# Turning the attention's q and k by VectorE blocks and DMA in place of TensorE transposes

## The chip, the core and the metric

The kernel runs on one core of one Trainium2 chip. The metric is the time of one launch on the device, in microseconds (us). The kernel before took 700.55 us (median of three runs, 700.42 to 700.56).

## What is computed

One layer over 512 tokens and 1024 channels in float32. The input is normalised and multiplied by one wide weight matrix; its columns are split among an mLSTM branch, a stick-breaking attention branch and the merge gates. Both branches are projected back, merged by the gates, and put through an output product.

```python
h = rmsnorm(x, norm_w)
proj = jnp.einsum('bsd,de->bse', h, w_in) + b_in
(mq, mk, mv, mi, mf, mo, mz, sq, sk, sv, sz, gates) = jnp.split(proj, split_at, axis=-1)
...
qs = rmsnorm(to_heads(sq, SB_HEADS), sb_q_norm_w)
ks_ = rmsnorm(to_heads(sk, SB_HEADS), sb_k_norm_w)
os_ = stick_breaking_attention(qs, ks_, to_heads(sv, SB_HEADS))
y_s = os_.transpose(0, 2, 1, 3).reshape(b_, s_, SB_WIDTH) * jax.nn.silu(sz)
...
merged = (g_m * jnp.einsum('bse,ed->bsd', y_m, w_proj_m)
          + g_s * jnp.einsum('bse,ed->bsd', y_s, w_proj_s))
x = x + jnp.einsum('bsd,de->bse', merged, w_out)
```

The attention has 8 heads of 128 channels. Its scores need q and k with the channel on the partitions (the contraction runs over partitions), while the input product leaves the tokens of q and k on the partitions. The turn from one to the other is what the change is about.

## The kernel before

**Units.** The dense work is a list of 118 units; the loop at L1199 runs them in order. A unit is one 512 KB piece of weights and its 24 matmuls: every product is made of three (`mm3`, L84), since both factors are split in a high and a low part. Two units ahead, `ahead` splits the weights: ACT copies the high part `wh` (L90), DVE subtracts to get the low part `wl` (L91). SP issues the loads of `stg`, four units ahead (L110), into three buffers. Around the two halves of a unit's matmuls the loop puts the evacuation of the unit before, functions put off with `defer(n, fn)` (they come up n units later), and one step of each active head. In the units listed in `REST` (11, 16, 20, 23, 24, ...) no head takes a step.

**Order of the groups.** The attention comes in two sets of four heads. Set 0: q in units 0 to 3, k 4 to 7, v 8 to 11, z 12 to 15. Set 1: q 16 to 19, k 20 to 23, z 24 to 27, v 28 to 31. Then two mLSTM pairs, pair 0 in units 32 to 51 (o, z, v, q, k) and pair 1 in 52 to 71, then gates, the two projections and the last product. A q or k group fills four PSUM banks (`dps`, one for each block of 128 tokens, of which there are four); after its fourth unit DVE moves the banks to `qraw` or `kraw` (L335, 128 tokens x 512 channels each), ACT squares them for the norm (`sqj`, L344), POOL makes the reciprocal root `rk` or `rq` (L267, L268), and DVE scales `kraw` by it (L355). There are four `dps` banks in all, so the next group's first matmul into a bank waits for that move.

**A head** (`head`, L383) is a generator: each `yield` ends a step. Step one turns q and k of the head with 8 TensorE transposes into PSUM (`aps`, L389) and splits them in high and low parts (L393, L394, L90, L91). The later steps make scores, weigh them (ACT sigmoids, POOL masks, DVE scans at L422 and products at L423 into `a_all`), transpose the weights in square blocks of 32 on DVE (`ay`, L440), move the blocks to their places with 16 DMAs issued by SP (`az<-ay`, L458), split them (`ath`, `atl`) and multiply them with v. A head begins when its unit in `SB_START` is reached and its set's k is marked done.

**Buffers.** `a_all` and `ay` share the tag "A", which has four buffers used in turn: a head's two tiles stand at two places, and the next but one head gets them again. Whoever fills a buffer waits for all who still read what was in it before; for `ay` these are its 16 `az` DMAs.

Of the kernel before, what the change touches and what calls it, by code (L numbers as in the profile page):

```python
# [34 lines left out]
def tile_hybrid_layer(  # L35
# [20 lines left out]
    def pool(name, bufs=1, **k):  # L56
# [11 lines left out]
    BUFS = {"stg": 3, "wh": 3, "wl": 3, "tmp": 2, "acc": 1, "om": 3, "P5": 2, "A": 4,  # L68
            "qk": 18, "vh": 5, "vl": 5, "y": 16, "brow": 1}

    MISC = {"om", "tmp", "acc", "brow", "stg"}

    def blk(tag, dt=F32, shape=(512,), name=None, p=128):

        where = mp if tag in MISC else sp
        return where.tile([p] + list(shape), dt, name=name or tag, tag=tag, bufs=BUFS[tag])

    def dense_ps():
# [233 lines left out]
    class SbSet:  # L312
        def __init__(self, s):
            self.s = s
            self.raw = {"q": [], "k": []}
            self.r = []
            self.v = []

        def z_group(self):
# [10 lines left out]
        def qk_group(self, name, c0):  # L330
            row = []

            def evac(tb, ps):
                t = blk("qk", name=name + "raw")
                nc.vector.tensor_tensor(t, ps, row[0], op=OP.add)  # L335
                self.raw[name].append(t)

                def norm():
                    ssq = tiny.tile([128, 4], F32, name="ssq", bufs=2)
                    rr = tiny.tile([128, 8], F32, name="r" + name, bufs=8 if name == "q" else 4)  # L340
                    r = rr[:, 0:4]
                    junk = blk("acc", BF, (128,), name="sqj")
                    for h in range(4):
                        nc.scalar.activation(junk, t[:, h * 128:(h + 1) * 128], AF.Square,  # L344
                                             accum_out=ssq[:, h:h + 1])
                    rstd(r, ssq, 128, EPS)
                    if name == "q":
                        rn = rr[:, 4:8]
                        nc.gpsimd.tensor_scalar(rn, r, -1.0, None, op0=OP.mult)
                        self.r.append((r, rn))  # L350
                    else:
                        def scale():
                            for h in range(4):
                                hs = slice(h * 128, (h + 1) * 128)
                                nc.vector.tensor_scalar(t[:, hs], t[:, hs], r[:, h:h + 1], None, op0=OP.mult)  # L355
# [27 lines left out]
        def head(self, h):  # L383
            hs = slice(h * 128, (h + 1) * 128)
            tr = []
            for name in ("q", "k"):
                tp = att_ps()
                for tb in range(TB):
                    nc.tensor.transpose(tp[:, tb * 128:(tb + 1) * 128], self.raw[name][tb][:, hs], ident)  # L389
                th = blk("qk", FR, name=name + "th")  # L390
                tl = blk("qk", FR, name=name + "tl")
                if name == "q":
# [4 lines left out]
                tr.append((th, tl))  # L397
            yield
# [217 lines left out]
    class MPair:  # L616
# [25 lines left out]
        def qk_group(self, name, c0, o):  # L642
            def evac(ct, ps):
# [12 lines left out]
                def mult():  # L656
# [3 lines left out]
                    def high():  # L660
                        th = blk("qk", FR, name="m%sh" % name)
                        tl = blk("qk", FR, name="m%sl" % name)
                        nc.scalar.activation(th, t, AF.Copy)
# [157 lines left out]
    for p in pairs:  # L821
        p.o_group()
        p.z_group()
        p.v_group()
        p.qk_group("q", C_MQ, 0)
        p.qk_group("k", C_MK, 8)

    gs_t, gm_t = [], []

    def gs_tile(ct):  # L830
        tag = ("brow", "om", "om", "acc", "qk")[min(ct, 4)]
        gs_t.append(blk(tag, shape=(516 if tag == "om" else 512,), name="gs")[:, 0:512])
        return gs_t[ct]

    def gm_tile(ct):
        gm_t.append(blk("qk", name="gm"))
        return gm_t[ct]
# [47 lines left out]

    merged = []

    def pm_evac(ct, ps):
# [3 lines left out]
        th = blk("y", FR, name="mgh")  # L892
        tl = blk("qk", FR, name="mgl")
        nc.scalar.activation(th, t, AF.Copy)
# [196 lines left out]
    def first_split(i, low=None):  # L1091
        u = units[i]
        for j in range(2):
            hi, lo = blk("qk", FR, name="fh"), blk("y", FR, name="fl")
            nc.scalar.activation(hi, u.st[:, j, :], AF.Copy)
# [12 lines left out]

    idle = blk("qk", FR, name="idle")
    nc.vector.memset(idle.bitcast(F32), 0.0)  # L1110
# [139 lines left out]
```

## Time and profile before

| | before |
|---|---|
| runs, median of 3 | 700.55 us (700.42 to 700.56) |
| the profiled execution's own time | 700.42 us |
| span of its profile | 698.7 us |
| POOL busy, instructions | 109.2 us, 249 |
| DMA moved | 80.94 MB in 104759 packets |
| `az<-ay` DMAs | 128 of 40 KB, 2.0 us to landing |

The profile is of one execution. A row of its timeline has the start in us from the span's beginning, the time taken, the engine, the line, the operation, what it writes and reads, and how many neighbours were merged; in brackets stands the idle time of the engine before it and who ended that. PE is TensorE, DVE is VectorE, ACT is ScalarE, POOL is GpSimd, SP is the engine that issues most DMAs. The chain of work that ended last is followed back from the last instruction: what stands on it sets the end. The 1.7 us between span and the execution's own time lie outside the profile.

### The profile page before, as it was taken

Reading aid. Unit: us, or ns where it says so; the run is one execution under the profiler, and the core shown is the slowest. Engines: PE = TensorE matmul, PEld = TensorE weight load, DVE = VectorE, ACT = ScalarE, POOL = GpSimd, SP = SyncE. Lnnn points to the kernel's source line nnn. Section 1 sums busy time; section 2 is a strip of 40 time slices with the busy share of each in tenths; the row PEclk is TensorE's granted clock in tenths of the full one; section 3 lists DMA queues with packets and bytes.
Section 4 is the critical chain, followed back from the end, with each engine's and each line's share of the span. In section 5 each row is a group of like instructions: output and inputs, shape, how many; then the busy total and the mean of one; then the engine's idle time right before and its main releaser. Section 6 shows DMA issues by size and latency. Waiting matters only on the chain.

```text
span 698.7 us, 9267 instructions
## 1 busy us (share of the span) xinstructions
PE 690.4 (99%) x3220; PEld 575.2 (82%) x3220; DVE 463.5 (66%) x807; ACT 335.6 (48%) x629; POOL 109.2 (16%) x249
## 2 busy tenths in 40 slices
PE   7999999999999999999999999999999999999997
PEld 5888888888888888888888888888888888888876
DVE  6837887856787775389944738995343364445996
ACT  6245354475554543244475534446563353344451
POOL 5422122252130220000011120001111000111021
PEclk9999999999999999999999999999999999999999
DMA  7432424525433444333332244433323456589434
GB/s 247 136 106 71 126 63 123 148 59 145 112 107 84 130 109 137 90 95 94 97 98 67 61 108 120 120 90 91 91 61 86 112 157 219 144 184 208 126 81 130
DMA packets 104759, 80.94 MB, mean 116 GB/s; under 512 B 6766, under 2 KB 89096, under 8 KB 104712
## 3 DMA queue, kind: packets, MB, share of 16 engines
q1 hardware_dynamic: 102552, 74.45, 37.2%
q0 software_dynamic: 2016, 5.77, 4.5%
q8 instruction: 25, 0.41, 0.2%
q14 instruction: 22, 0.18, 0.1%
q10 hardware_dynamic: 144, 0.13, 0.1%
HBM read 65.12 MB, written 2.10 MB: 96 GB/s over the span
## 4 chain that ended last, share of the span: by engine, by line
PE 97%; DMA 1%; DVE 1%; POOL 0%; SPq 0%; issue 0%; ACT 0%; DVEq 0%
PE dps L85 27%; PE dps L86 27%; PE dps L87 27%; PE aps L86 3%; PE aps L87 3%; PE aps L85 3%; PE aps L389 1%; PE dps L1139 1%; PE dps L1137 1%; PE dps L1138 1%; DMA stg<-in_w_in_dram 1%; PE aps L760 1%; PE aps L762 1%; PE aps L761 1%; DVE fl L1096 0%; POOL fl L1096 0%
## 5 line engine op out<-in xcount | busy, mean ns | idle before, releaser
L91 DVE TENSOR_TENSOR wl<-stg,wh 128x1024 fp32r<-128x1024 f32 x92 | 112.6, 1223 | 112.9 <-ACT wh L90 111.3
L85 PE MATMUL dps<-hh,wh 128*128 128x512 f32 x448 | 175.2, 391 | 0.0
L87 PE MATMUL dps<-hh,wl 128*128 128x512 f32 x448 | 174.5, 389 | 0.0
L86 PE MATMUL dps<-hl,wh 128*128 128x512 f32 x448 | 174.5, 389 | 0.0
L90 ACT ACTIVATE wh<-stg 128x1024 fp32r<-128x1024 f32 x92 | 96.8, 1052 | 58.4 <-PE dps L87 38.2
L87 PEld LDWEIGHTS dps<-hh,wl 128*128 128x128 f32 x448 | 84.1, 188 | 17.8
L85 PEld LDWEIGHTS dps<-hh,wh 128*128 128x128 f32 x448 | 84.1, 188 | 17.1 <-DVE tmp L372 0.4
L86 PEld LDWEIGHTS dps<-hl,wh 128*128 128x128 f32 x448 | 84.2, 188 | 16.9
L85 PE MATMUL dps<-wh,hh 128*128 128x512 f32 x224 | 88.2, 394 | 0.1
L87 PE MATMUL dps<-wh,hl 128*128 128x512 f32 x224 | 87.3, 390 | 0.0
L86 PE MATMUL dps<-wl,hh 128*128 128x512 f32 x224 | 87.3, 390 | 0.0
L87 PEld LDWEIGHTS dps<-wh,hl 128*128 128x128 f32 x224 | 42.0, 188 | 9.0
L85 PEld LDWEIGHTS dps<-wh,hh 128*128 128x128 f32 x224 | 42.1, 188 | 8.6 <-issue 0.5
L86 PEld LDWEIGHTS dps<-wl,hh 128*128 128x128 f32 x224 | 42.1, 188 | 8.1
L651 DVE SCALAR_TENSOR_TENSOR acc<-tmp,vec,acc 128x511 f32<-128x511 f32 (+2 forms) x48 | 36.0, 750 | 1.7
L654 ACT ACTIVATE tmp<-acc 128x512 f32<-128x512 f32 x16 | 10.1, 633 | 50.8 <-DVE acc L651 50.8
L422 DVE TENSOR_TENSOR_SCAN om<-om 128x512 f32<-128x512 f32 (+3 forms) x32 | 26.7, 835 | 8.8 <-POOL om L416 8.8
L416 POOL TENSOR_SCALAR_AFFINE_SELECT om<-om 128x128 f32<-128x128 f32 x32 | 14.1, 441 | 109.0 <-ACT om L414 109.0
L713 POOL TENSOR_SCALAR_AFFINE_SELECT w_all<-om 128x128 f32<-128x128 f32 x16 | 6.0, 412 | 153.9 <-DVE om L708 136.8
L414 ACT ACTIVATE om<-aps,rq 128x512 f32<-128x512 f32 (+3 forms) x32 | 16.8, 525 | 22.8 <-PE aps L87 22.8
L85 PE MATMUL dps<-yh,wh 128*128 128x512 f32 x64 | 24.9, 389 | 0.0
L86 PE MATMUL dps<-yl,wh 128*128 128x512 f32 x64 | 24.9, 389 | 0.0
(271 smaller groups left out, 1225.3 us busy)
## 6 DMA issues: line engine op xcount, KB each, us to landing
stg<-in_w_in_dram SPq DMA_DIRECT2D x87, 512.0 KB, 3.8
az<-ay SPq DMA_DIRECT2D x128, 40.0 KB, 2.0
stg<-in_w_proj_s_dram SPq DMA_DIRECT2D x8, 512.0 KB, 3.7
B<-in_w_out_dram SPq DMA_DIRECT2D x8, 512.0 KB, 4.8
stg<-in_w_proj_m_dram SPq DMA_DIRECT2D x8, 512.0 KB, 3.6
wl<-stg POOLq DMA_DIRECT2D x8, 512.0 KB, 5.5
brow<-in_b_in_dram SPq DMA_DIRECT2D x8, 256.0 KB, 4.0
hz<-ht SPq DMA_DIRECT2D x64, 32.0 KB, 1.9
```

The costliest lines, as they stand in the source:

```text
L85: nc.tensor.matmul(ps, ah, bh, start=first, stop=False)
L86: nc.tensor.matmul(ps, ah, bl, start=False, stop=False)
L87: nc.tensor.matmul(ps, al, bh, start=False, stop=last)
L90: nc.scalar.activation(hi, src, AF.Copy)
L91: nc.vector.tensor_tensor(lo, src, hi.bitcast(F32), op=OP.subtract)
L389: nc.tensor.transpose(tp[:, tb * 128:(tb + 1) * 128], self.raw[name][tb][:, hs], ident)
L414: nc.scalar.activation(om[:, 0:n], zp, AF.Sigmoid, scale=rn[:, h:h + 1])
L416: nc.gpsimd.affine_select(out=om[:, ts], in_=om[:, ts], compare_op=OP.is_gt, fill=1.0, base=0, channel_multiplier=1, pattern=[[-1, 128]])
L422: nc.vector.tensor_tensor_scan(back, back, back, 1.0, op0=OP.mult, op1=OP.bypass)
L651: nc.vector.scalar_tensor_tensor(acc[:, j:], t[:, 0:T - j], cw(3 - j, ch), acc[:, j:], op0=OP.mult, op1=OP.add)
L654: nc.scalar.activation(t, acc, AF.Sigmoid)
L760: nc.tensor.matmul(nm[:, 0:258], ph, vh, start=j == 0, stop=False)
```

## The change

For q of both sets and k of set 1 (`TURNED`) the TensorE transposes go. In their place a new function `turn` runs for each of the four token blocks: two DVE transposes in square blocks of 32 write into two tiles `ty` of the tag "A"; after the fourth block, 32 DMAs of 32 KB carry the blocks to their places in `tz`, eight in each of four units that follow. In set 0 SP issues them all, in set 1 SP and POOL issue half each. The head then reads `tz` where it read PSUM; q is multiplied by the norm weight in place, once for two heads. k of set 0 keeps its TensorE transposes. The heads of set 1 begin in units 31, 33, 36, 39 in place of 26, 28, 31, 34 (the first one waits for k to be marked done, in unit 32), and pair 0's v group comes behind its q and k. The tag "qk" now has buffers of twice the size, half as many.

```diff
-SB_START = [10, 13, 16, 19, 26, 28, 31, 34]
+SB_START = [10, 13, 16, 19, 31, 33, 36, 39]
+TURNED = {("q", 0), ("q", 1), ("k", 1)}
...
-            "qk": 18, "vh": 5, "vl": 5, "y": 16, "brow": 1}
+            "qk": 9, "vh": 5, "vl": 5, "y": 16, "brow": 1}
...
+                        if tb % 2:
+                            defer(1, lambda: self.turn(name, tb - 1))
+                            defer(1, lambda: self.turn(name, tb))
...
-                            if tb == TB - 1:
+                            if (name, self.s) in TURNED:
+                                self.turn(name, tb)
+                            elif tb == TB - 1:
                                 done.add(("k", self.s))
...
+        def turn(self, name, tb):
+            if tb == 0:
+                self.ty[name] = [sp.tile([128, 8, TB, 32], F32, name="ty", tag="A", bufs=4) for _ in range(2)]
+            ty = self.ty[name]
+            for g in range(2):
+                nc.vector.transpose(ty[g][:, :, tb, :],
+                                    self.raw[name][tb][:, 256 * g:256 * g + 256].rearrange("p (x j) -> p x j", j=32))
+            if tb < TB - 1:
+                return
+            tz = self.tz[name] = [None, None]
+            def move(g, bs):
+                if tz[g] is None:
+                    tz[g] = blk("qk", F32, (2, 4, 128), name="tz")
+                src = ty[g].rearrange("p (h b) i j -> p b h (i j)", h=2)
+                for b in bs:
+                    for a in range(4):
+                        q = nc.gpsimd if self.s and a % 2 else nc.sync
+                        q.dma_start(tz[g][32 * b:32 * b + 32, :, a, :], src[32 * a:32 * a + 32, b])
+                if name == "k" and g == 1 and bs[-1] == 3:
+                    defer(2, lambda: done.add(("k", self.s)))
+            for n, (g, bs) in enumerate([(0, (0, 1)), (0, (2, 3)), (1, (0, 1)), (1, (2, 3))]):
+                defer(1 + n, lambda g=g, bs=bs: move(g, bs))
...
+                if (name, self.s) in TURNED:
+                    tp = self.tz[name][h // 2][:, h % 2].rearrange("p a (i j) -> p i a j", j=32)
+                    th, tl = [x.rearrange("p (i a j) -> p i a j", a=4, j=32) for x in own]
+                    if name == "q" and h % 2 == 0:
+                        z = self.tz[name][h // 2]
+                        nc.vector.tensor_scalar(z, z, qkw, None, op0=OP.mult)
+                else:
+                    tp = att_ps()
+                    for tb in range(TB):
+                        nc.tensor.transpose(tp[:, tb * 128:(tb + 1) * 128], self.raw[name][tb][:, hs], ident)
...
-        p.v_group()
+        if p.p:
+            p.v_group()
         p.qk_group("q", C_MQ, 0)
         p.qk_group("k", C_MK, 8)
+        if not p.p:
+            p.v_group()
```

Below, rows are in each engine's program order; a number behind a name tells tiles apart, and what an instruction waits for stands in brackets (DMAHW: a lane of DMAs issued by SP, DMASW: one of those issued by POOL).

The first place is DVE's queue in units 22 and 23. In it are the first block transposes of head 3's weights (`ay`), the scans and products behind them, the low part of unit 25's weights, and the first move of set 1's k out of PSUM. Before:

```order
L91 TENSOR_TENSOR atl_1688<-az_1372,ath_1687 128x384 [waits Activation_49]
L440 STREAM_TRANSPOSE ay_1699<-a_all_1612 128x4x32 x4
L440 STREAM_TRANSPOSE ay_1699<-a_all_1612 128x4x32 [waits DVE_49]
L422 SCALAR_TENSOR_TENSOR om_1709<-om_1709 128x256 [waits Pool_49]
L423 TENSOR_TENSOR a_all_1612<-a_all_1612,om_1709 128x256 [waits DVE_49,Pool_49]
L422 SCALAR_TENSOR_TENSOR om_1719<-om_1719 128x384 [waits Pool_49]
L423 TENSOR_TENSOR a_all_1612<-a_all_1612,om_1719 128x384 [waits DVE_49,Pool_49]
L91 TENSOR_TENSOR wl_1742<-stg_1578,wh_1741 128x1024 [waits DMAHW1_49,Activation_49]
L335 TENSOR_TENSOR kraw_1771<-dps_1526,brow_1656 128x512 [waits DMAHW2_49,PE_49]
```

Now, in the same place:

```order
L97 TENSOR_TENSOR atl_1706<-az_1389,ath_1705 128x384 [waits Activation_49]
L490 STREAM_TRANSPOSE ay_1717<-a_all_1626 128x4x32 [waits DMAHW4_49,DMAHW5_49,DMAHW3_49,DMAHW6_49,DMAHW2_49,DMAHW7_49,DMAHW1_49,DMAHW0_49]
L490 STREAM_TRANSPOSE ay_1717<-a_all_1626 128x4x32 x3
L490 STREAM_TRANSPOSE ay_1717<-a_all_1626 128x4x32 [waits DVE_49]
L472 SCALAR_TENSOR_TENSOR om_1727<-om_1727 128x256 [waits Pool_49]
L473 TENSOR_TENSOR a_all_1626<-a_all_1626,om_1727 128x256 [waits DVE_49,Pool_49]
L472 SCALAR_TENSOR_TENSOR om_1737<-om_1737 128x384 [waits Pool_49]
L473 TENSOR_TENSOR a_all_1626<-a_all_1626,om_1737 128x384 [waits DVE_49,Pool_49]
L97 TENSOR_TENSOR wl_1769<-stg_1592,wh_1768 128x1024 [waits Activation_49]
L346 TENSOR_TENSOR kraw_1798<-dps_1534,brow_1670 128x512 [waits PE_49]
```

The rows stand in the same order, but the first `ay` has got a wait on all eight lanes. Set 1's two `ty` tiles of q took the next two places of the tag "A" between head 2 and head 3, so head 3's `ay` gets the buffer of head 2's `ay`, and waits for that head's 16 `az` DMAs.

The second place is DVE's queue in unit 25: the scaling of the first two blocks of set 1's k, and behind it the low part of unit 27's weights. Before, and then now:

```order
L355 TENSOR_SCALAR kraw_1771<-kraw_1771,rk_1774 128x128 [waits DVE_49,Pool_49]
L355 TENSOR_SCALAR kraw_1771<-kraw_1771,rk_1774 128x128 x3
L355 TENSOR_SCALAR kraw_1782<-kraw_1782,rk_1785 128x128 [waits DVE_49,Pool_49]
L355 TENSOR_SCALAR kraw_1782<-kraw_1782,rk_1785 128x128 x3
L91 TENSOR_TENSOR wl_1859<-stg_1745,wh_1858 128x1024 [waits DMAHW4_49,PE_49,Activation_49]
```

```order
L369 TENSOR_SCALAR kraw_1798<-kraw_1798,rk_1801 128x128 x3
L391 STREAM_TRANSPOSE ty_1878<-kraw_1798 128x8x32 [waits DMASW7_49,DMAHW1_49,DMASW6_49,DMAHW2_49,DMASW5_49,DMAHW3_49,DMASW4_49,DMAHW4_49,DMASW3_49,DMAHW5_49,DMASW2_49,DMAHW6_49,DMASW1_49,DMAHW7_49,DMASW0_49,DVE_49]
L391 STREAM_TRANSPOSE ty_1879<-kraw_1798 128x8x32 [waits DMASW7_49,DMAHW0_49,DMASW6_49,DMAHW1_49,DMASW5_49,DMAHW3_49,DMASW4_49,DMAHW4_49,DMASW3_49,DMAHW5_49,DMASW2_49,DMAHW6_49,DMASW1_49,DMAHW7_49,DMASW0_49,DVE_49]
L369 TENSOR_SCALAR kraw_1798<-kraw_1798,rk_1811 128x128 [waits Pool_49]
L369 TENSOR_SCALAR kraw_1798<-kraw_1798,rk_1811 128x128 x3
L391 STREAM_TRANSPOSE ty_1878<-kraw_1798 128x8x32 [waits DVE_49]
L391 STREAM_TRANSPOSE ty_1879<-kraw_1798 128x8x32 [waits DVE_49]
L97 TENSOR_TENSOR wl_1907<-stg_1772,wh_1906 128x1024 [waits PE_49,Activation_49]
```

Four block transposes stand between the scaling and the weights. The two `ty` tiles of k take the buffers of the two `ty` tiles of q, so the first transpose into each waits until q's DMAs out of it have landed, those of POOL included.

The third place is POOL's queue in units 25 and 26, as it is now; before, only the four pairs of `rk` rows stood there. `tz_1865` is the second of the two turned tiles of set 1's q. Ahead of these rows stand four DMAs of the first tile, the `rk` rows of k's first two blocks, and four more DMAs.

```order
L404 DMA tz_1865<-ty_1563 32x2x128 [waits DMASW0_49,DVE_49,PE_49]
L404 DMA tz_1865<-ty_1563 32x2x128 [waits DMASW1_49]
L404 DMA tz_1865<-ty_1563 32x2x128 [waits DMASW2_49]
L404 DMA tz_1865<-ty_1563 32x2x128 [waits DMASW3_49]
L273 TENSOR_SCALAR rk_1889<-ssq_1888 128x4 [waits Activation_49]
L274 TENSOR_TENSOR rk_1889<-rk_1889,mhalf_89 128x4 [waits Pool_49]
L273 TENSOR_SCALAR rk_1898<-ssq_1897 128x4 [waits Activation_49]
L274 TENSOR_TENSOR rk_1898<-rk_1898,mhalf_89 128x4 [waits Pool_49]
L404 DMA tz_1865<-ty_1563 32x2x128 [waits DMASW4_49]
L404 DMA tz_1865<-ty_1563 32x2x128 [waits DMASW5_49]
L404 DMA tz_1865<-ty_1563 32x2x128 [waits DMASW6_49]
L404 DMA tz_1865<-ty_1563 32x2x128 [waits DMASW7_49]
```

The last four DMAs of q (DMASW4 to 7) stand behind the norms of k's third and fourth block, and those wait for ACT.

More of the change, by code (lines that the diff above doesn't have):

```diff
@@ L331, in qk_group @@
             row = []
+            half = []
             def evac(tb, ps):
-                t = blk("qk", name=name + "raw")
+                if tb % 2 == 0:
+                    half.extend(two("qk", name=name + "raw"))
+                t = half[tb]
                 nc.vector.tensor_tensor(t, ps, row[0], op=OP.add)
@@ L386, in head @@
             for name in ("q", "k"):
[L387 to L392, printed above, removed]
+                th, tl = own = two("qk", FR, name=name + "tt")
+                if (name, self.s) in TURNED:
[8 more added lines that the diff above has]
+                        nc.tensor.transpose(tp[:, tb * 128:(tb + 1) * 128], self.raw[name][tb][:, hs], ident)
+                if name == "q" and not (name, self.s) in TURNED:
                     nc.scalar.activation(th, tp, AF.Copy, scale=qkw)
@@ L396, in head @@
                     split(tp, th, tl)
-                tr.append((th, tl))
+                tr.append(own)
             yield
@@ L886, in tile_hybrid_layer @@
     merged = []
+    mgl = []
     def pm_evac(ct, ps):
@@ L892, in pm_evac @@
         th = blk("y", FR, name="mgh")
-        tl = blk("qk", FR, name="mgl")
+        if ct % 2 == 0:
+            mgl.extend(two("qk", FR, name="mgl"))
+        tl = mgl[ct]
         nc.scalar.activation(th, t, AF.Copy)
@@ L1107, in tile_hybrid_layer @@
     load_vecs()
-    idle = blk("qk", FR, name="idle")
+    idle = two("qk", FR, name="idle")[0]
     nc.vector.memset(idle.bitcast(F32), 0.0)
```

20 lines of the change are left out of this document (14 added, 6 removed).

## The prediction, before the changed kernel was run

> **What bounds the kernel now.** I read the page's busy shares first, then the chain that ended last, then the timeline of DVE, SP and POOL where the order of the queues changes.
>
> ```profile
> PE 690.4 (99%) x3220; PEld 575.2 (82%) x3220; DVE 463.5 (66%) x807; ACT 335.6 (48%) x629; POOL 109.2 (16%) x249
> PE 97%; DMA 1%; DVE 1%; POOL 0%; SPq 0%; issue 0%; ACT 0%; DVEq 0%
> ```
>
> TensorE is busy 99% of the span and is 97% of the chain. So a matmul that goes is worth what it takes on that chain, and an instant in which TensorE has to wait is lost in full: nothing later makes it up. The transposes stand on the chain as eight pieces, one for each head:
>
> ```profile
> 77.85 1.02 PE aps L389 x8
> 97.14 0.87 PE aps L389 x8
> 116.32 0.88 PE aps L389 x8
> 135.49 0.87 PE aps L389 x8
> 180.54 0.90 PE aps L389 x8
> 196.23 0.87 PE aps L389 x8
> 217.28 0.90 PE aps L389 x8
> 236.69 0.87 PE aps L389 x8
> ```
>
> **The part that goes.** Set 1's heads lose all eight transposes: 0.90 + 0.87 + 0.90 + 0.87 = 3.54 us. Set 0's lose q's four of eight, half of 1.02 + 0.87 + 0.88 + 0.87, 1.82 us. **Together 5.36 us**, 0.11 us for each of 48.
>
> ```profile
> L389 PE MATMUL aps<-ident,qraw 128*128 128x128 f32 x32 | 4.9, 275 | 0.0
> ```
>
> One transpose lasts 275 ns, but they run into one another, and the chain has 0.11 us of each. I count the chain's. The Trainium skill (VectorE: DVE Perf Modes, section "The three transpose paths") puts a 128x128 transpose at 390 ns on TensorE and 311 ns on VectorE, which only turns blocks of 32; the rules at the end of that page give the 128x128 case to TensorE. TensorE: Matmul & The Clock Gate, Part 4, has 275 ns in one kernel, and by 275 ns the 48 would be worth 13.2 us; the row's duration agrees, and the chain says that it is not what a transpose costs here.
>
> **What is added, and beside what it lies.** The nearest rows for the new DVE work:
>
> ```profile
> L780 DVE STREAM_TRANSPOSE ht<-hns 128x256 f32<-128x256 f32 x16 | 6.6, 430 | 3.1 <-PE aps L761 3.1
> L283 DVE TENSOR_SCALAR x<-x,xs 128x1024 f32<-128x1024 f32 x4 | 3.3, 848 | 0.6 <-POOL xs L268 0.5
> ```
>
> 24 block transposes of 128x256 at 0.43 us are 10.3 us, four scalings of 128x1024 at 0.85 us are 3.4 us. DVE is idle a third of the span, so 13.7 us has room, and TensorE pays nothing where the weights' low part still comes in time. SP issues 64 more DMAs, of some 0.59 us as `az` below: 8 in a unit are 4.7 us, in set 0 within a unit of 5.44 us, with loads issued four units ahead. In set 0 I cost all of this at nothing; if that cover failed, it would be by less than a microsecond. What counts is where the new work makes DVE **wait**, since in DVE's queue stand the weights and the moves that empty PSUM.
>
> **First wait: head 3's `ay`, unit 22.** It now waits for head 2's 16 `az` DMAs. In the profile of before, the same stretch of SP and DVE:
>
> ```profile
> 155.63 6.85 SPq L458 DMA_DIRECT2D az<-ay  x8
> L458 SPq DMA_DIRECT2D az<-ay x128: 507/588/1646, 104.8 to 271.9; - x128
> DMA to landing us min/median/max: 1.8/2.0/6.5
> 158.00 1.08 DVE L440 STREAM_TRANSPOSE ay<-a_all 128x128 f32<-128x128 f32 x5
> 159.00 0.65 DVE L422 TENSOR_TENSOR_SCAN om<-om 128x256 f32<-128x256 f32 x1
> ...
> 161.63 1.22 DVE L91 TENSOR_TENSOR wl<-stg,wh 128x1024 fp32r<-128x1024 f32 x1
> 162.77 1.88 DVE L335 TENSOR_TENSOR kraw<-dps,brow 128x512 f32<-128x512 f32 x3
> 165.10 0.69 DVE L335 TENSOR_TENSOR kraw<-dps,brow 128x512 f32<-128x512 f32 x1 [0.45 <-PE dps L87]
> 164.90 0.39 PE L85 MATMUL dps<-hh,wh 128*128 128x512 f32 x1
> ```
>
> Head 2's second eight DMAs are issued from 155.63 to 162.48, the last of them near 161.9; with 2.0 us to landing (the median of `az`) head 2's buffer is free at 163.9. DVE got to its `ay` at 158.00. All that follows on DVE moves by 5.9 us: from the start of `ay` to that of the scans 1.00, to the weights 2.63, to `kraw` 1.14, and a `kraw` takes 0.69, as the fourth row has it. So the first bank is empty at 163.9 + 1.00 + 2.63 + 1.14 + 0.69 = 169.36. TensorE wants that bank at 164.90, where unit 24 begins (the matmuls change their form there). **A stall of 4.46 us.** The earlier transposes that went move SP and TensorE alike, so the difference stays. Its bounds: with the shortest landing, 1.8, it is 4.3; if the last DMA landed at 6.5, the longest, it is 9. Behind the waiting row stand unit 25's and 26's weights too, but they have a unit's time more.
>
> **Second wait: set 1's k, unit 25.** The first turns of k wait for q's moves, and POOL has 16 of these to issue. What POOL takes for one, no row shows; the nearest two kinds are:
>
> ```profile
> L119 POOL DMA_DIRECT2D wl<-stg x8 | 7.1, 893 | 93.5 <-DVE yml L91 61.7 <-ACT wl L118 27.5 <-DVE B L938 4.3
> L1019 POOL DMA_DIRECT2D xr<-u x6 | 5.3, 1028 | 40.6 <-ACT u L1027 22.3 <-DVE u L1036 10.8 <-DVE u L1047 7.5
> ```
>
> Both go over 128 partitions; the new ones go over 32, in 64 runs of 512 bytes. Half of 0.893 is the lower end, 0.45 us, 1.03 the upper. I take 0.89, as the two kinds differ in bytes (512 and 256 KB) and not downward with them. The Trainium skill (DMA: Bandwidth & Descriptors, "Latency and other measured facts") says about 1 us to the first byte for DMAs issued from GpSimd, which would make eight of them 0.9 us longer; no run here shows it for this size.
>
> The other rows are these of k's norm and of DVE:
>
> ```profile
> 163.49 0.31 ACT L344 ACTIVATE sqj<-kraw 128x128 bf16<-128x128 f32 x1 [2.77 <-DVE kraw L335]
> ...
> 167.30 1.01 POOL L268 TENSOR_TENSOR rk<-rk,mhalf 128x4 f32<-128x4 f32 x1
> ...
> 171.13 0.30 ACT L344 ACTIVATE sqj<-kraw 128x128 bf16<-128x128 f32 x1
> ...
> 174.98 1.01 POOL L268 TENSOR_TENSOR rk<-rk,mhalf 128x4 f32<-128x4 f32 x1
> 170.34 0.39 PE L85 MATMUL dps<-hh,wh 128*128 128x512 f32 x1
> 177.02 0.39 PE L85 MATMUL dps<-hh,wh 128*128 128x512 f32 x1
> 184.06 0.39 PE L85 MATMUL dps<-hh,wh 128*128 128x512 f32 x1
> 175.60 1.23 DVE L91 TENSOR_TENSOR wl<-stg,wh 128x1024 fp32r<-128x1024 f32 x1 [1.98 <-ACT wh L90]
> 178.84 1.65 DVE L355 TENSOR_SCALAR kraw<-kraw,rk 128x128 f32<-128x128 f32 x8
> ```
>
> Units 24 to 27 begin at 164.90, 170.34, 177.02 and 184.06. With the first stall unit 24 begins at 169.36, 25 at 174.8, 26 at 181.5; unit 26 has no head to begin any more and lasts 7.04 - 0.90 = 6.14, so 27 begins at 187.6. POOL: k's first two norms end 168.31 - 163.49 = 4.82 us after the first `kraw`, at 174.2. Eight DMAs (the second and third four) at 0.89 end at 181.3. The next two norms could end at 169.36 + 5.44 + 0.80 (ACT's first piece behind the beginning of unit 25, 171.13 - 170.34) + 4.86 (175.99 - 171.13) = 180.5, so they run behind the eight DMAs, 2.5 us, to 183.8. The last four go out by 187.4, and land by 189 (2.0 us after the last is issued at 186.5 to 187.4). Only then does DVE make its second `ty` of k: 0.43, four scalings 0.83 (half of 1.65), two transposes 0.86, and unit 27's weights 1.14: 192.3. **A stall of 192.3 - 187.6 = 4.7 us.** With 0.45 a DMA the third four end by 177.8, the norms at 182.3 at the latest, the last lands by 186, and the weights are there at 189 less what DVE didn't wait; about the time at which they are wanted: 0 to 1 us. With 1.03, twelve DMAs are 1.7 us later: 6.4.
>
> In unit 28 DVE has 7.0 us of rows up to the next weights (the five `ay` rows, two splits and evacuations as before, eight scalings 1.65, four transposes 1.72, weights 1.14), TensorE some 6.6 (a unit without heads takes 170.34 - 164.90 = 5.44; head 3's products fill the rest): another 0.4 us.
>
> **The moved heads.** Set 1's heads take their DVE work from units 26 to 45 to units 32 to 50, where pair 0's q and k are convolved. First, what DVE did for two of these heads where they stood, then how full DVE was in the units from 32 on, and in the convolutions among them:
>
> ```profile
> L422 DVE TENSOR_TENSOR_SCAN om<-om 128x512 f32<-128x512 f32 (+3 forms) x8 | 6.6, 831 | 2.8 <-POOL om L416 2.8
> L440 DVE STREAM_TRANSPOSE ay<-a_all 128x128 f32<-128x128 f32 x20 | 4.3, 274 | 0.0
> L423 DVE TENSOR_TENSOR a_all<-a_all,om 128x512 f32<-128x512 f32 (+3 forms) x8 | 4.1, 516 | 0.9
> 221.00:343.00 122.00, 122.00 (x563) 102.08 (x564) 89.55 (x135) 54.73 (x85) 8.52 (x27) 1.00 0.38 102
> 299.00:343.00 44.00, 44.00 (x196) 36.45 (x195) 38.22 (x51) 19.92 (x29) 0.00 (x0) 1.00 0.33 86
> 302.82 1.23 DVE L91 TENSOR_TENSOR wl<-stg,wh 128x1024 fp32r<-128x1024 f32 x1 [0.25 <-ACT wh L90]
> 309.80 0.39 PE L85 MATMUL dps<-hh,wh 128*128 128x512 f32 x1
> ```
>
> The 15.0 us of scans, block transposes and products come into a stretch in which DVE is idle for 122.0 - 89.6 = 32.4 us, so they fit. Within the eight convolution units DVE is idle for only 44.0 - 38.2 = 5.8 us, but the weights lie ahead there by 309.80 - 304.05 = 5.75 us at the least: 11.5 us of cover for the 7.5 us of one head. I cost it at nothing; a second head within these units would cost 15.0 - 11.5 = 3.5 us.
>
> **The sum** goes against the profiled execution's own 700.42 (span 698.7, 1.7 outside it; the median is 700.55, 0.13 above): 700.42 - 5.36 + 4.46 + 4.7 + 0.4 = **704.6 us**.
>
> **The rivals.**
>
> *Only one wait reaches TensorE.* If POOL issues such a small DMA in half the time, the second stall is gone: 700.42 - 5.36 + 4.46 = 699.5. If instead `az` lands early enough for `kraw`, the second alone is 3.2 + 0.4 (all begins 4.46 earlier, but k's turn hangs less on ACT): 698.7. For it speaks that half as many runs are sent; against it, that the rows don't fall with size. 26%.
>
> *A clean removal.* Both waits end under cover: 700.42 - 5.36 = 695.1. For it speaks that weights lie well ahead (5.75 us at the convolutions); against it, that `kraw` had only 164.90 - 163.46 = 1.4 us to spare and now gets 5.9 us later. 10%.
>
> *DVE falls behind in the convolutions* on top of both stalls, from the point where two heads' scans and products fall into these eight units, with the 3.5 us above: 708.1, slower. Against it speaks that a head also lengthens TensorE's units. 12%.
>
> *A transpose is worth its full 275 ns*, 13.2 us in all, with both stalls: 700.42 - 13.2 + 9.6 = 696.8. For it speaks only the duration, against it the chain's 0.9 us for eight. 5%.
>
> The forecast keeps 47%.
>
> **How the numbers follow.** 704.6 is the likeliest case; by the bounds of POOL's price (0.45 to 1.03) and of `az`'s landing it alone reaches from 700.42 - 5.36 + 4.3 + 0.4 = 699.8 to 704.6 + 4.5 = 709.1. The range is 697.0 to 709.5: below, it leaves out the clean removal and the cheapest full-price case; above, the larger half of a DVE that falls behind. About 0.2% (1.4 us) is what a measurement of this kernel can tell from no change. Slower by more than that: the forecast, 47, the DVE rival, 12, and 2 of a single, larger stall: 61. Faster by more (under 699.1): clean removal 10, full price 5, a single smaller stall 8: 23. Between: 16.
>
> **What would show it.** Right: TensorE idle some 4 us ahead of unit 24's first matmul, ended by DVE's `kraw`; DVE idle ahead of head 3's first `ay`, ended by an `az` DMA; TensorE idle ahead of unit 27, ended by DVE's low weights, and DVE idle ahead of `ty` from `kraw`, ended by a POOL DMA; POOL's `tz` rows near 0.9 us; no transposes of q. Wrong: POOL's rows near 0.45 us and no gap at unit 27; DVE's `ay` of head 3 without idle time; gaps of TensorE in units 40 to 48, where I see none; or the chain's pieces of L389 larger in what they free than 5.4 us.

## The result, and the profile after

The changed kernel takes **718.04 us** (median of 6 runs, 717.14 to 719.03) against 700.55 (6 runs, 700.0 to 701.24) for the one before: ratio 1.0249, interval 1.0236 to 1.0263. The forecast of slower held; its size did not: 17.5 us in place of 4.1. The profiled execution is one of 718.69, with a span of 717.0.

The page's busy shares, and the chain's shares by engine, for the changed kernel:

```profile
PE 693.1 (97%) x3172; PEld 574.4 (80%) x3172; DVE 472.8 (66%) x835; ACT 334.8 (47%) x629; POOL 125.8 (18%) x281
PE 65%; issue 4%; DVE 3%; ACT 1%; POOL 1%; DMA 0%; SPq 0%; DVEq 0%; POOLq 0%; ACTq 0%
```

The 48 transposes have gone (3220 matmuls less 3172). TensorE is busy for 2.7 us *more* all the same, though it has less to do: some of its matmuls got longer. And the chain, which was TensorE's by 97%, is now its by 65%. Who holds TensorE up stands in its longest waits (total, times, longest one):

```profile
PE aps L91 <- ACT ath L96: 6.5, 2, 4.9
PE dps L91 <- DVE kraw L346: 4.8, 1, 4.8
PE aps L92 <- DVE atl L97: 3.8, 2, 3.6
```

To place the loss I laid this trace beside that of the run `e12_all_waits_gone` below, which has TensorE's same matmuls and none of these waits (696.59 in the profiled execution). A unit's length is from its first matmul to the next unit's; a slow matmul is one that begins 0.43 us after the one before it where 0.23 is usual. Nearly all units agree to 0.05 us. These don't (idle is the time by which the next matmul begins later for want of its operands; the rows of waits above count up to 0.2 us less):

| units | after | without the waits | more | idle | slow matmuls | what TensorE waited for |
|---|---|---|---|---|---|---|
| 23 and 24 | 18.33 | 10.88 | 7.45 | 4.95 | 12 | DVE's `kraw` |
| 26 | 11.62 | 6.17 | 5.45 | 3.65 | 8 | DVE's `atl` of head 3 |
| 42 | 8.50 | 6.17 | 2.33 | 1.74 | 1 | ACT's `ath` |
| 46 | 13.77 | 6.17 | 7.60 | 5.09 | 9 | ACT's `ath` |

Together 22.83 us: 15.43 idle, and 7.4 in which TensorE works slowly afterwards. From unit 4 to unit 105 the run without waits is 4.27 us shorter than the kernel before. 22.83 - 4.27 is 18.56, the two executions differ by 718.69 - 700.42 = 18.27, and what lies ahead of unit 4 makes up the other 0.3.

The slow matmuls show in the windows of the waits and of what comes behind them. A row has the stretch, then its length and the busy time of PE, PEld, DVE, ACT and POOL with counts, the granted clock, DMA share and GB/s:

```profile
163.10:168.30 5.20, 0.41 (x3) 0.09 (x1) 4.99 (x11) 0.18 (x1) 0.00 (x0) 0.82 0.51 128
168.30:176.20 7.90, 7.90 (x25) 6.28 (x26) 2.81 (x4) 3.99 (x17) 5.69 (x11) 0.68 0.49 118
185.60:189.50 3.90, 0.30 (x3) 0.04 (x1) 3.55 (x10) 0.03 (x1) 0.00 (x0) 1.00 0.00 0
189.50:194.50 5.00, 5.00 (x18) 4.08 (x19) 5.00 (x19) 0.00 (x0) 0.60 (x2) 0.66 0.48 146
320.30:325.60 5.30, 0.36 (x3) 0.05 (x1) 4.60 (x7) 2.23 (x5) 0.00 (x0) 0.80 0.44 126
325.60:331.50 5.90, 5.88 (x18) 4.72 (x19) 5.79 (x9) 2.61 (x5) 0.00 (x0) 0.60 0.30 89
```

They go in pairs. In the first of each TensorE does almost nothing; in the second it is busy throughout, at a granted clock of 0.60 to 0.68. Before, the mean clock of the whole execution was 1.000.

**The two early waits**, in DVE's timeline (start, time taken, what; in brackets the idle time before and who ended it):

```profile
162.44 1.28 DVE L490 STREAM_TRANSPOSE ay<-a_all 128x128 f32<-128x128 f32 x5 [5.96 <-DMA tz<-ty]
...
166.27 1.22 DVE L97 TENSOR_TENSOR wl<-stg,wh 128x1024 fp32r<-128x1024 f32 x1
167.41 2.48 DVE L346 TENSOR_TENSOR kraw<-dps,brow 128x512 f32<-128x512 f32 x4
...
185.95 0.45 DVE L391 STREAM_TRANSPOSE ty<-kraw 128x256 f32<-128x256 f32 x1 [6.32 <-DMA tz<-ty]
...
187.75 1.18 DVE L97 TENSOR_TENSOR wl<-stg,wh 128x1024 fp32r<-128x1024 f32 x1
188.85 0.55 DVE L97 TENSOR_TENSOR atl<-az,ath 128x384 fp32r<-128x384 f32 x1
```

DVE stands still for 5.96 us ahead of head 3's `ay`, and `kraw` begins 5.0 us after it. (The row blames a `tz` DMA; the order shows that `ay` waits for DMA lanes that `az` and `tz` share. The trace has head 2's last `az` landing at 162.16, 0.3 us before `ay` begins. In `e11` below the same wait is put down to `az<-ay`, which landed at 161.52, again 0.3 us before.) DVE stands still again for 6.32 us ahead of k's second `ty`. What TensorE misses after it is `atl`, the low part of head 3's weights, which stands in the queue behind that `ty`, the rest of that scaling and turning, and unit 27's weights (`wl`). Who made that DMA late stands in POOL's timeline, with the group of all its new DMAs (count | busy, mean ns) below it:

```profile
172.90 4.31 POOL L404 DMA_DIRECT2D tz<-ty  x8
178.76 0.18 POOL L273 TENSOR_SCALAR rk<-ssq 128x4 f32<-128x4 f32 x1 [1.56 <-ACT sqj L355]
179.03 1.03 POOL L274 TENSOR_TENSOR rk<-rk,mhalf 128x4 f32<-128x4 f32 x1
180.54 0.20 POOL L273 TENSOR_SCALAR rk<-ssq 128x4 f32<-128x4 f32 x1 [0.48 <-ACT sqj L355]
180.82 1.01 POOL L274 TENSOR_TENSOR rk<-rk,mhalf 128x4 f32<-128x4 f32 x1
181.79 2.21 POOL L404 DMA_DIRECT2D tz<-ty  x4
```

```profile
L404 POOL DMA_DIRECT2D tz<-ty x32 | 17.3, 549 | 10.1 <-DVE ty L391 9.9 <-issue 0.2
```

The last four DMAs left from 181.79 on, at once behind the norm (`rk`) of k's fourth block. Between the eight and that norm POOL had only the norm of the third block to do, and stood idle for 1.56 and 0.48 us: it waited for ACT, not for its own DMAs.

**The late waits** stand on the chain, here around unit 46 (start, the us for which the piece stands on the chain, what; the last three rows are TensorE's matmuls behind the wait, slow and then at full speed):

```profile
322.04 0.76 DVE acc L701
322.83 0.76 DVE acc L701
323.61 0.76 DVE acc L701
324.45 0.07 ACT tmp L704
324.99 0.52 ACT ath L96
325.55 0.58 PE aps L91
...
328.01 0.43 PE dps L92
...
330.74 0.23 PE dps L93
```

`acc` are the taps of pair 0's convolution on DVE, `tmp` is the sigmoid on ACT that needs them, and `ath` is the high part of a set-1 head's weights, which stands behind that sigmoid in ACT's queue. It is DVE that is late. These are the first and the last of five such rows of DVE:

```profile
300.88 1.22 DVE L97 TENSOR_TENSOR wl<-stg,wh 128x1024 fp32r<-128x1024 f32 x1
...
326.61 1.22 DVE L97 TENSOR_TENSOR wl<-stg,wh 128x1024 fp32r<-128x1024 f32 x1
```

Four periods in 25.73 us, 6.43 us a unit; DVE was busy for 23.65 of them, 5.91 a unit. In the run without waits, units 42 to 46 took TensorE 29.90 us, 5.98 each. The change brought the two together from both sides: the heads begin later, and with the v group behind q and k the convolutions of pair 0 come four units sooner. No run separates the two.

### The profile page after: what moved, and what is told of

The parts are those of the page before. It is cut to its first block, busy times and chain, and to the rows that moved or that the text cites. A ratio compares the mean times of both kernels' runs of the same rounds, so it can differ in the third digit from the quotient of the medians.

```text
span 717.0 us, 9374 instructions
## 1 busy us (share of the span) xinstructions
PE 693.1 (97%) x3172; PEld 574.4 (80%) x3172; DVE 472.8 (66%) x835; ACT 334.8 (47%) x629; POOL 125.8 (18%) x281
## 4 chain that ended last, share of the span: by engine, by line
PE 65%; issue 4%; DVE 3%; ACT 1%; POOL 1%; DMA 0%; SPq 0%; DVEq 0%; POOLq 0%; ACTq 0%
PE dps L91 19%; PE dps L93 19%; PE dps L92 19%; PE aps L92 2%; PE aps L93 2%; PE aps L91 2%; DVE acc L701 1%; PE aps L809 1%; PE aps L811 1%; PE aps L810 1%; SPq L508 0%; DVE om L472 0%; DVE wl L97 0%; DVE acc L699 0%; DMA az<-ay 0%
## 5 line engine op out<-in xcount | busy, mean ns | idle before, releaser
L91 PE MATMUL dps<-hh,wh 128*128 128x512 f32 x448 | 177.4, 396 | 4.8 <-DVE kraw L346 4.8
L92 PE MATMUL dps<-hl,wh 128*128 128x512 f32 x448 | 176.6, 394 | 0.0
L93 PE MATMUL dps<-hh,wl 128*128 128x512 f32 x448 | 176.6, 394 | 0.0
L91 PEld LDWEIGHTS dps<-hh,wh 128*128 128x128 f32 x448 | 85.7, 191 | 22.3 <-issue 5.2
L93 PE MATMUL dps<-yh,wl 128*128 128x512 f32 x64 | 24.9, 389 | 0.0
```

The lines of the kernel that those rows point to most:

```text
L91: nc.tensor.matmul(ps, ah, bh, start=first, stop=False)
L92: nc.tensor.matmul(ps, ah, bl, start=False, stop=False)
L93: nc.tensor.matmul(ps, al, bh, start=False, stop=last)
```

## The experiments

Times are medians; each ratio is against runs of the kernel before on the same chip. Edits are of the changed kernel unless said otherwise.

### Does head 3's `ay` cause the first wait?

```diff
-SB_START = [10, 13, 16, 19, 31, 33, 36, 39]
+SB_START = [10, 13, 16, 21, 31, 33, 36, 39]
```

> The changed kernel with head 3 of set 0 beginning in unit 21 in place of 19, so that its ay tile is filled in unit 25 and takes a buffer that q's turned tiles held, and k's first turned tile takes head 2's ay buffer. Theory (the stalls at units 24 and 26 are waits for a buffer of the tag A, handed down through DVE's queue): both go, with the slow matmuls behind each: 718.0 less 7.5 (4.95 idle and 2.5 slow) less 5.5 (3.65 idle and 1.8 slow), about 705. Rival (DVE is simply too full there: the 24 turns and the scalings): the stalls stay or move by a unit, 715 to 718.

**720.76 us, 1.0288 (1.0274 to 1.0302)** (`e1`): the theory's number was missed by 16 us, and the rival's 715 to 718 by 3. The gap ahead of unit 24 went, as it said, but head 3's `ay` now stands one place on in the tag "A", on q's second tile. DVE's rows there:

```profile
180.16 1.08 DVE L490 STREAM_TRANSPOSE ay<-a_all 128x128 f32<-128x128 f32 x5 [4.73 <-issue]
...
189.06 1.14 DVE L97 TENSOR_TENSOR atl<-az,ath 128x512 fp32r<-128x512 f32 x2
```

```profile
PE aps L92 <- DVE atl L97: 5.3, 3, 4.9
PE aps L91 <- ACT ath L96: 4.9, 2, 3.3
PE aps L91 <- ACT ktt L96: 4.4, 1, 4.4
```

`ay` waits for q's last POOL DMAs (landed at 179.49), and `atl` comes 4.9 us too late. The other 4.4 us, for head 4's `ktt` in unit 33, come from a different tag. Ahead of `ktt` in ACT's queue stands the high part of v's last block:

```profile
228.19 0.63 ACT L419 ACTIVATE vh<-tmp 128x512 fp32r<-128x512 f32 x1 [8.39 <-PE aps L92]
```

`vh` has five buffers, and this one waits for a product of head 3, which begins only at 227.76 now that head 3 is two units later; DVE's scaling of `tz` and ACT's `ktt` (232.26) follow. So a later start of head 3 only chooses who waits: the tag "A" has four buffers, too few for the order, and `vh` five.

### The moves out of q's tiles, in two units in place of four

```diff
-                defer(1 + n, lambda g=g, bs=bs: move(g, bs))
+                defer(1 + (n // 2 if self.s and name == "q" else n), lambda g=g, bs=bs: move(g, bs))
```

> The changed kernel with set 1's q moved by DMA in two units (16 DMAs in each) in place of four. Theory (at unit 26 the last four POOL DMAs of q stand behind the norms of k's third and fourth block in POOL's queue, and those wait for ACT): the last DMAs go out ahead of these norms, near 177 in place of 184, the wait of k's second turned tile ends by 181, the stall of 5.5 us at unit 26 goes and that at unit 24 stays: about 712.5. Rival (what POOL takes for a DMA, 0.53 us, or the landing, 3 us, sets it): less than 2 us gained, 716 to 718.

**712.76 us, 1.0176 (1.0161 to 1.0192)** (`e2`). As expected. DVE's rows, against 185.95 and 188.85 above:

```profile
179.62 0.45 DVE L391 STREAM_TRANSPOSE ty<-kraw 128x256 f32<-128x256 f32 x1 [0.67 <-issue]
...
182.53 0.55 DVE L97 TENSOR_TENSOR atl<-az,ath 128x384 fp32r<-128x384 f32 x1
```

Issued ahead of the two late norms, the same DMAs cost TensorE no wait: 5.3 us are back. So what cost was how late they left, which their place in POOL's queue decided, and not POOL's price for one.

### DVE's work in the convolutions

```diff
-                for j in (1, 2, 3):
+                for j in ():
```

This leaves out three of the convolution's four taps.

> The changed kernel with three of the four taps of the mLSTM's convolution left out: 2.3 us less of DVE in each of 16 units. Theory (from unit 40 on DVE is behind with heads 6 and 7 and the convolutions together; ACT's ath stands behind an ACT row that waits for DVE's taps): the stalls of units 41, 42 and 46, some 10 us with the slow matmuls, go: about 707 to 708. Rival (TensorE waits there for the az DMAs or for ACT itself): 715 to 718.

**707.84 us, 1.0106 (1.0092 to 1.012)** (`e3`). As expected. The waits of units 42 and 46 are gone, the two early ones stay. The 10.2 us stand for 9.93 in the table.

### Buffers of their own for the `ty` tiles

```diff
-                self.ty[name] = [sp.tile([128, 8, TB, 32], F32, name="ty", tag="A", bufs=4) for _ in range(2)]
+                self.ty[name] = [blk("qk", F32, (8, TB, 32), name="ty") for _ in range(2)]
```

> The changed kernel with the ty tiles taken from the tag qk instead of A, so that neither head 3's ay nor k's turned tiles wait for a buffer. Theory (the stalls at units 24 and 26 are waits for a buffer of A): both go, and nothing new takes their place near units 27 or 33; the stalls of units 41, 42 and 46 stay: 718.0 less 7.5 and 5.5, about 705. Rival (the turned tiles merely need the time; the wait reappears a unit or more later, as with head 3 moved): 712 or more.

**706.1 us, 1.0077 (1.0063 to 1.009)** (`e5`), 1 us above the theory's number and 6 below the rival's. The new buffers are those of the tag "qk", which other tiles use in turn too. Both early waits go with one line, 11.9 us for the 12.90 of the table, and the late ones stay.

### All of them at once

The two edits above together; three taps are left out here too.

```diff
-                self.ty[name] = [sp.tile([128, 8, TB, 32], F32, name="ty", tag="A", bufs=4) for _ in range(2)]
+                self.ty[name] = [blk("qk", F32, (8, TB, 32), name="ty") for _ in range(2)]
...
-                for j in (1, 2, 3):
+                for j in ():
```

> The changed kernel with the ty tiles in the tag qk and three of the four taps of the mLSTM's convolution left out. Theory (the waits at units 24 and 26 and those of units 41 to 46 are all that the change costs): 48 transposes less and no wait but the 0.6 us in unit 19, 700.5 less 5.4 plus 0.6, 695 to 696. Rival (something else costs, spread over the run): 698 or more.

**696.39 us, 0.9938 (0.9924 to 0.9953)** (`e12`), 0.4 us above what was expected and 1.6 below the rival's bound; the page's line on the engines:

```profile
PE 685.5 (99%) x3172; PEld 570.0 (82%) x3172; DVE 437.1 (63%) x787; ACT 335.8 (48%) x629; POOL 124.8 (18%) x281
```

TensorE is back at 99%, and is busy for 7.6 us less than after with the same 3172 matmuls: that is the slow clock's part. Two causes, the shared tag and DVE's load in the convolutions, account for all that was lost: alone they gave 11.9 and 10.2 us, together 21.65.

### Is the slow clock the wait's, or the change's?

Here the kernel **before** gets rows of DVE that do nothing of use, in its order ahead of the `kraw` that unit 24 waits for: 16 in one run, 28 in the other.

```diff
+        if c == 23:
+            for _ in range(16):
+                nc.vector.tensor_scalar(rb2[64:128, 0:128], rb2[64:128, 0:128].bitcast(F32), 1.0, None, op0=OP.mult)
```

> The kernel before, with 16 added DVE rows (some 0.21 us each, 3.4 us) ahead of k's first move out of PSUM in unit 24. TensorE waits there about 2 us (3.4 less the 1.4 that the move had to spare). Theory (only a wait of some 4 us and more makes the matmuls after it slow): the time grows by the wait alone, 702.4. Rival (every wait is followed by slow matmuls): 704 or more.

> The kernel before, with 28 added DVE rows (5.9 us) at the same place; TensorE waits about 4.5 us. Theory (after such a wait the matmuls run at 0.43 us apiece in place of 0.23, for some 12 of them, whatever made the wait): the time grows by the wait and about 2.4 us more, 700.4 + 4.5 + 2.4, about 707.3, with a granted clock below 1 in that stretch. Rival (the slow matmuls belong to the turned tiles, their DMAs or DVE's work beside TensorE): the wait alone, 704.9.

**704.26 us, 1.0054 (1.0037 to 1.0071) (`e6`), and 708.89, 1.0112 (1.0099 to 1.0126) (`e7`).** The rows took 224 ns each, 3.6 and 6.3 us, and TensorE stood idle for 2.95 and 6.06 us. The windows of the small delay, and then of the large one:

```profile
164.50:167.60 3.10, 0.32 (x2) 0.02 (x1) 2.79 (x11) 0.10 (x1) 0.00 (x0) 0.87 0.93 314
167.60:176.00 8.40, 8.39 (x25) 6.65 (x25) 2.88 (x4) 4.06 (x17) 2.42 (x4) 0.64 0.19 60
```

```profile
165.00:171.20 6.20, 0.30 (x2) 0.03 (x1) 5.48 (x23) 0.11 (x1) 0.00 (x0) 0.68 0.29 103
171.20:178.10 6.90, 6.90 (x25) 5.61 (x26) 2.87 (x4) 4.06 (x17) 2.42 (x4) 0.79 0.04 6
```

A wait alone, with no transposes turned, brings the clock of 0.64 to 0.79 behind it. In the traces the small delay is followed by 14 slow matmuls and costs 5.9 us up to unit 25, twice its idle time; the large one by 7, and costs 7.5. The large delay's 708.89 is 1.6 us above the theory's number, since TensorE waited for 6.06 us and not 4.5; the rival's 704.9 is out. My price for the small one missed: its time lies on the rival's side, 704. Its four runs explain themselves, since each lists its mean clock: 706.52 at 0.995 (the profiled one), 704.80 at 0.997, 703.63 and 703.71 at 1.000. The last two are 3.0 and 3.1 us above the kernel before, which is the wait alone. After 2.95 us of idleness the slow stretch comes in some executions and not in others; after 6.06 us all four runs stood at 0.995. The Trainium skill (TensorE: Matmul & The Clock Gate, "Part 1: The HAM clock gate (the "warmup" mystery)") says that a free-running window of about 3.4 us decides, half the clock after an idle one and full clock after a busy one, so that the count of slow matmuls changes from run to run. The spread just told agrees, and so does unit 42 of `e1`, where most of the slow matmuls begin only 2.0 us after the wait. But waits of 2.95 and 1.75 us are shorter than such a window, and that they bring the slow clock does not follow from the rule alone. The Trainium skill's section "Why this matters for your kernels", on the same page, asks for no gaps over about 3 us. Here that bound isn't safe: in the runs `e1` and `e5` the wait of 1.75 us at unit 42 had 10 and 7 slow matmuls behind it, where the changed kernel had 1.

### All moves issued by SP

```diff
-                        q = nc.gpsimd if self.s and a % 2 else nc.sync
+                        q = nc.sync
```

> The changed kernel with all of set 1's moves issued by SP, none by POOL. Theory (at unit 26 only POOL's last four DMAs are late, since they stand behind norms that wait for ACT; SP's own four went out at 174 to 177): with eight at SP the last goes out near 179 and lands by 182, 4 us earlier than the 186 of POOL's, and the stall at unit 26 nearly goes: 712.5 to 714. Rival (the moves as such are too many in the time, whoever issues them): 717 or more.

**719.41 us, 1.0273 (1.0252 to 1.0294)** (`e11`): the rival's number was right. POOL's queue is out of the matter, but SP takes longer. Its rows, and then two of DVE:

```profile
172.03 5.06 SPq L404 DMA_DIRECT2D tz<-ty  x8
177.76 5.06 SPq L404 DMA_DIRECT2D tz<-ty  x8
```

```profile
161.79 1.29 DVE L490 STREAM_TRANSPOSE ay<-a_all 128x128 f32<-128x128 f32 x5 [4.83 <-DMA az<-ay]
...
184.29 0.45 DVE L391 STREAM_TRANSPOSE ty<-kraw 128x256 f32<-128x256 f32 x1 [6.75 <-DMA tz<-ty]
```

The last eight go out from 177.76 to 182.8, and k's second `ty` begins at 184.29, 1.7 us sooner than with POOL. TensorE is there sooner too, since the first wait was shorter, and by its row still waits 3.4 us for `atl`, where it was 3.6. Together with `e2` this says that the DMAs must leave sooner; another engine for them is not enough. And here the first wait bears its own name, `az<-ay`.

### What of the change can be kept

**q alone**, k by TensorE again; the order of the groups and set 1's heads as before, head 3 two units later:

```diff
-SB_START = [10, 13, 16, 19, 31, 33, 36, 39]
+SB_START = [10, 13, 16, 21, 26, 28, 31, 34]
-TURNED = {("q", 0), ("q", 1), ("k", 1)}
+TURNED = {("q", 0), ("q", 1)}
```

> q of both sets turned, k of both left to TensorE; heads of set 1 begin at 26, 28, 31, 34 and pair 0's groups stand as before the change, head 3 begins in unit 21. Theory (a turn is free where no queue waits for it): no stall of TensorE, 32 transposes of 0.11 us less: 700.5 less 3.6, about 697. Rival (DVE's 16 turns and 64 DMAs cost by themselves): 700 or more.

**699.47 us (11 runs), 0.9984 (0.9975 to 0.9993)** (`e4`): 2.5 us short of what was expected. In the profiled run, the slowest of the eleven at 700.50, TensorE waits 1.0 us in unit 26 for DVE's scaling of k, and 1.3 us near the end for a load of weights.

**q alone, with the `ty` tiles in "qk"** and all starts as before:

```diff
-SB_START = [10, 13, 16, 19, 31, 33, 36, 39]
+SB_START = [10, 13, 16, 19, 26, 28, 31, 34]
-TURNED = {("q", 0), ("q", 1), ("k", 1)}
+TURNED = {("q", 0), ("q", 1)}
...
+                self.ty[name] = [blk("qk", F32, (8, TB, 32), name="ty") for _ in range(2)]
```

> q of both sets turned with the ty tiles in the tag qk; k left to TensorE, heads and groups where they were before the change. Theory: no wait for a buffer and no lateness of the heads; 32 transposes of 0.11 us less, 700.4 less 3.6, about 697, with TensorE idle for less than 0.5 us between units 10 and 60. Rival (64 SP and POOL DMAs and 16 turns cost something of their own, as the 1.2 us in unit 26 of the run with head 3 moved may say): 699 to 700.

**700.55 us (11 runs), 1.0001 (0.9991 to 1.0011)** (`e8`): no gain, where 697 was expected and 699 to 700 by the rival. The early waits are gone, but a small one stood up in unit 31:

```profile
216.79 0.71 DVE L437 TENSOR_SCALAR tz<-tz,qkw 128x1024 f32<-128x1024 f32 x1
218.20 0.69 DVE L97 TENSOR_TENSOR qtt<-tz,qtt 128x512 fp32r<-128x512 f32 x1 [0.70 <-ACT qtt L96]
...
219.41 1.28 DVE L416 TENSOR_TENSOR tmp<-dps,brow 128x512 f32<-128x512 f32 x2
```

DVE scales `tz`, waits 0.70 us for ACT's high part of it, makes the low part, and only then empties v's banks (`tmp`). TensorE waits 1.93 us for those. There is a second loss in this trace: its last matmul ends 1.07 us ahead of the kernel before (693.73 against 694.80), but the rest behind it takes 4.91 us in place of 3.90, after DVE stood 1.23 us for a DMA `xr<-u` at 683.01. Whether that belongs to the change is open. The scaling, then, was moved to two units behind the DMAs, and out of the head:

```diff
+                if name == "q" and bs[-1] == 3:
+                    defer(2, lambda: nc.vector.tensor_scalar(tz[g], tz[g], qkw, None, op0=OP.mult))
...
-                    if name == "q" and h % 2 == 0:
-                        z = self.tz[name][h // 2]
-                        nc.vector.tensor_scalar(z, z, qkw, None, op0=OP.mult)
```

> q of both sets turned, ty in the tag qk, heads and groups as before the change; the scaling of tz by the norm weight is done two units after its DMAs, not in the head's first step. Theory (in the run without it, unit 31's 1.9 us of idle TensorE come from DVE scaling, ACT copying and DVE subtracting one after the other ahead of the moves of v out of PSUM): that wait goes, and with it the time falls to 700.5 less some 3, about 697.5. Rival (DVE is too full at that place in any case): 699 to 700.5.

**698.92 us (11 runs, 698.08 to 700.34), 0.9974 (0.9965 to 0.9983)** (`e9`). The theory's 697.5 was not reached, and the time is at the edge of the rival's range. The wait of unit 31 shrinks to 0.48. This is the fastest version that computes the whole layer, and beats both kernels: 0.26% less than before.

**The whole change with every edit**: own buffers, early scaling, set 1's moves in two units, and its heads begun in units 29, 31, 33 and 35, ahead of the convolutions:

```diff
-SB_START = [10, 13, 16, 19, 31, 33, 36, 39]
+SB_START = [10, 13, 16, 19, 29, 31, 33, 35]
...
-                defer(1 + n, lambda g=g, bs=bs: move(g, bs))
+                defer(1 + (n // 2 if self.s else n), lambda g=g, bs=bs: move(g, bs))
```

> The whole change (48 transposes gone), ty in the tag qk, tz scaled early, set 1's DMAs in two units in place of four, and set 1's heads in units 29, 31, 33, 35. Theory (the last 10 us come from heads 6 and 7 beside the convolutions of units 40 to 47; earlier they lie beside the lighter o and z groups): no wait above 2 us from unit 40 on, 700.5 less 5.4 plus at most 3, so 695 to 698. Rival (pair 0's convolutions in units 40 to 47 are too much for DVE with any head near): 702 or more.

**707.68 us, 1.01 (1.0087 to 1.0114)** (`e10`): a miss by 10 us. The rival's number held, but not its place. TensorE's waits say where it went:

```profile
PE aps L92 <- DVE ktt L97: 3.0, 2, 2.6
PE dps L91 <- DVE tmp L418: 2.5, 1, 2.5
PE aps L91 <- ACT ath L96: 0.8, 2, 0.5
```

The late waits (`ath`) are nearly gone, and others have taken their place, in unit 31 (v's banks, `tmp`) and unit 36 (a head's `ktt`, with 8 slow matmuls behind it). In both places tried for these heads with all 48 transposes turned, DVE reaches something late.

## Why the prediction was wrong in size, step by step

**The part that goes: right, a tenth too large.** Predicted 5.36 us. From the kernel before to the run without waits it was 4.27, and a gap of 0.56 stands against it in unit 19, where TensorE waits for `qraw`: the transposes freed 4.8. (Gaps of 0.1 to 0.4 us in both traces, in units 19, 31, 32 and 41, nearly cancel.) That is 0.10 us each: the chain's 0.11 was near, the row's 275 ns was not.

**First wait: right, in part by luck.** The cause, the place and the engine are those named, and 4.46 us was predicted where 4.95 was measured. `ay` began at 162.44, against 163.9 less the 1.6 us saved by then. Two terms behind that 163.9 were off and cancelled: head 2's last `az` was issued at 158.89, not at 161.9 less 1.6, and took 3.27 us to land, not 2.0.

**Second wait: the cause right, its terms not.** 4.7 + 0.4 were predicted, 3.65 measured. Two terms were off. POOL takes 0.55 us for such a DMA, not 0.89; by the text's own lower bound the wait should then have been 0 to 1 us. It was larger because the consumer was wrong: TensorE did not wait for unit 27's weights but sooner, in unit 26, for head 3's `atl`, which stands in the same DVE queue one row behind them. The 0.4 us of unit 28 did not come: units 27 and 28 took TensorE as long as in the run without waits. The order of POOL's queue, four DMAs behind two norms that wait for ACT, decided the time, as the prediction had it for the cheap case.

**The moved heads, "I cost it at nothing": the step that failed.** It compared DVE's extra work with the lead of the *weights*, and the weights were in time. What was late was something with no such lead: a head's `ath`, which TensorE needs within its unit, and which stands in ACT's queue behind a sigmoid that waits for DVE's convolution. As DVE took 6.43 us a unit in the convolutions, 5.91 of it busy, its lateness went through ACT to TensorE: 1.74 and 5.09 us idle, 9.93 with the slow clock. Such gaps in units 40 to 48 are on the prediction's own list of what would show it wrong. The rival named "DVE falls behind in the convolutions" had the place and the engine, at 12% and 3.5 us; it expected the weights there too, and two heads at a time. `e3` shows that DVE's load is the cause.

**The clock: not in the prediction at all.** This is the second step that failed. Each wait was priced at its idle time. Behind the waits of units 24, 26 and 46 TensorE worked at 0.60 to 0.68 of its clock for 5 us and more, and 7.4 us were lost so.

With the measured terms, against the profiled 718.69: 700.42 - 4.8 + 0.56 + 4.95 + 3.65 + 1.74 + 5.09 + 7.4 = 719.0; the rest is the 0.3 ahead of unit 4. Of the 14 us between the forecast and this execution, 7.4 are the clock and 6.8 the moved heads. The small ones cancel.

## What to carry to other kernels

Where a tile joins a tag that others use in turn, write down who gets which buffer and what the last reader waits for; other buffers for `ty` removed here in one line what moving a start only handed on. When work is added to an engine, don't ask whether the product with the longest lead still comes in time, but which product is needed soonest, and follow it through the queues of the other engines too, since a row that waits holds up all that stand behind it. And a wait of TensorE that lasts about 2 us or longer may cost up to 3 us on top, for the slow matmuls behind it.

## What the hardware showed beyond that

A DMA of 32 KB in 64 runs of 512 bytes took POOL 0.55 us to issue, where its 256 KB and 512 KB ones, over 128 partitions, took 1.03 and 0.89. So the small one over 32 partitions is the cheaper; whether its size or its partitions make it so, nothing here separates. SP took 0.63 us for each of the same DMAs, so that POOL was no slower at them.

The price of a wait is not a function of its length alone: 2.95 us idle cost up to 5.9, 6.06 us cost 7.5, and 1.75 us was followed by anything from 1 to 10 slow matmuls. What sets the count in a given execution is open.
